# Two one-number tiles take 64-byte homes in a decoder block's SBUF

## The chip, the cores and the metric

The kernel runs on one core of a Trainium2 chip. The metric is the device time of one execution in microseconds (us), as the median of several runs. The kernel before takes 746.96 us (three runs, 746.91 to 747.18).

## What is computed

One decoder block for 512 tokens of width 1024, in float32, cut here to what matters:

```python
h = rms_norm(x, g_mix)
u, q, k, v, gate_logits = split(h @ w_in)              # 512, 512, 512, 512, 1024 columns
y_pool = causal_multiscale_pool(u, w_pool, pool_scale)
o = diff_attention(rope(q), rope(k), v, lam)           # 4 heads, two softmaxes each, subtracted
y_attn = rms_norm(o, g_subln) * (1.0 - lam_init)
x = x + (concat(y_pool, y_attn) * sigmoid(gate_logits)) @ w_out
x = x + memory_cross_attention(rms_norm(x, g_cross), rms_norm(mem, g_mem))   # 256 memory rows
x = x + square(relu(rms_norm(x, g_mlp) @ w_up)) @ w_down                     # 1024 -> 4096 -> 1024
return rms_norm(x, g_final)
```

## The kernel before, in words

Activations stand transposed, features on the 128 partitions and the 512 tokens along the free dimension. Every large product is made from a high and a low float32r part of each operand. `mm3(o, lh, ll, rh, rl)` issues three matmuls into one PSUM tile (L94, L95, L96): high times high, high times low, low times high. In `nc.tensor.matmul(o, a, b)`, `a` is the stationary block (128 x 128) that TensorE loads into its array, and `b` is the moving tile that streams through it (512 columns mostly, 256 in some stages). `tile_mm` makes one output tile of 128 features from eight blocks of the contraction, so with 24 matmuls. In the mixers' input projections, the output projections and the MLP, the stationary operands are weight blocks: loaded into `wraw` by DMA, split by ScalarE (L100) into `whi` and by VectorE (L101) into `wlo`, three buffers each, always ahead of use.

The moving operands have homes by stage:

- q, k, gates and pooling input (until 171 us): `xg`, the scaled input.
- output projection of the mixers (from 171 us): `mix`.
- keys from the memory, `mem_k`: the normed memory in tiles of the tag `s`, 256 columns wide. Values from the memory, `mem_v`, turn it round: `s` is stationary and the weight block `whi` or `wlo` moves.
- cross attention: the query projection moves `xg`; scores have `s` stationary and `mix` moving, 256 columns wide; the products with the values have `mix` stationary and `at` moving.
- its output projection: `xg`. The first half of each MLP group ("up", eight tiles, 192 matmuls): `mix`. The second half ("down", eight tiles, 192 matmuls): `xg`. There are four such groups, one after the other, to the end.

TensorE's instructions keep the order in which the code issues them. Tiles come from one pool. `sb(tag, shape, bufs)` gives a tag `bufs` homes in a row; the homes stand in order of first use, and each is rounded up to 32 bytes per partition. So a tile of one float takes 32 bytes, and moves all that stands behind it by 32. `eps` (one float, the bias of each norm's logarithm) stands behind `vx`, `cst` and `tmp`; `gsub` (one float per partition, a gain of the attention's norm) stands behind `vr` and `lam`. In the built program the first byte of each tag, within a partition, is:

```
tag           bytes of a home   before, mod 64   mod 128   after, mod 64   mod 128
cst, tmp      6912, 2048              0              64           0             64
eps           32 (after: 64)          0               0           0              0
one_f, ones   512                    32              96           0              0
ss, wraw      2048, 4096             32              96           0              0
xg            4096                   32              96           0              0
whi, wlo      4096                   32              96           0              0
rstd          2048                   32              96           0              0
vr            2048                   32              32           0             64
gsub          32 (after: 64)         32              32           0              0
s             4096                    0               0           0             64
at            8192                    0               0           0             64
mix           4096                    0               0           0             64
```

All homes of one of these tags share the remainder, and so do their halves and the 128-column blocks in them, since these are multiples of 512 bytes apart.

Of the kernel before, what the change touches and what calls it, by code (L numbers as in the profile page):

```python
# [17 lines left out]
P = 128  # L18
# [9 lines left out]
EPS = 1e-6  # L28
# [18 lines left out]
def block_kernel(ctx: ExitStack, tc: tile.TileContext, x0g, xT, memT, wv, wm, wckv, wpool, vecs, csts, outT):  # L47
# [14 lines left out]
    def nm(s):  # L62
        uid[0] += 1
        return f"{s}_{uid[0]}"

    def sb(tag, shape, bufs, dt=F32):
        return pool.tile(shape, dt, tag=tag, name=nm(tag), bufs=bufs)

    def tmp(dt=F32):
        return sb("tmp", [P, T], 10, dt)  # L70
# [7 lines left out]
    def ps(tag, bufs):  # L78
        return psum.tile([P, T], F32, tag=tag, name=nm(tag), bufs=bufs)
# [7 lines left out]
    V = nc.vector  # L87
# [25 lines left out]
    warm = ps("acc", 2)  # L113
    for j in range(WARM):
        nc.tensor.matmul(warm, idle[:, :P], idle, start=j == 0, stop=j == WARM - 1)
    eps = sb("eps", [P, 1], 1)
    V.memset(eps, EPS)
    one_f = sb("onef", [P, P], 1)
    V.memset(one_f, 1.0)
    ones = sb("ones", [P, P], 1, F32R)  # L120
    V.tensor_copy(ones, one_f)

# [1 line left out]
    blocks = []  # L124

    def add(src):
# [35 lines left out]
            prep(j)  # L162
        return ready.pop(i)

# [1 line left out]
    def rsqrt(dst, ssum, scale, v, l, by=None):  # L166
        """dst = (ssum * scale + EPS) ** -0.5, times by(y) for a first factor; v and l are scratch"""
        V.tensor_scalar(v, ssum, scale, EPS, op0=ALU.mult, op1=ALU.add)
        S.activation(l, ssum, AF.Ln, bias=eps, scale=scale)
        S.activation(dst, l, AF.Exp, scale=-0.5)  # L170
        S.activation(l, dst, AF.Square)
        V.scalar_tensor_tensor(l, l, -0.5, v, op0=ALU.mult, op1=ALU.mult)
        if by is not None:
            by(dst)
        V.scalar_tensor_tensor(dst, l, 1.5, dst, op0=ALU.add, op1=ALU.mult)
# [38 lines left out]
        S.activation(hi, src, AF.Copy, scale=g)  # L214
        V.scalar_tensor_tensor(lo, src, g, f(hi), op0=ALU.mult, op1=ALU.subtract)

# [1 line left out]
    clock = [0]  # L218
    due = []

# [24 lines left out]
                first and n == 0, last and n == len(ks) - 1)  # L245
            tick()

# [1 line left out]
    WU, WQ, WK, WGATE, WOUT, WCQ, WCO = 0, 4, 8, 12, 20, 28, 36  # L249
    WUP = 44  # L250
    WDN = WUP + 32
# [25 lines left out]
    def W(*key):  # L277
        return weights(where[key])

# [1 line left out]
    xr = {0: vx[:, NG_COL:]}  # L281
    xg = {}
    ss = sb("ss", [P, T], 1)
# [18 lines left out]
            load(k // 2)  # L302
    nc.sync.dma_start(cst, csts)

# [1 line left out]
    def lambdas():  # L306
        lvec = tmp()[:, :NVEC]
        nc.gpsimd.dma_start(lvec, vecs)
        lam = sb("lam", [P, 4], 1)
        lsum = sb("lsum", [P, 4], 1)  # L310
        for j in range(2):
            b = 128 * j
            V.tensor_tensor(lvec[:, b:b + 64], lvec[:, b:b + 64], lvec[:, b + 64:b + 128], op=ALU.mult)
            V.tensor_reduce(lsum[:, j:j + 1], lvec[:, b:b + 64], axis=AX.X, op=ALU.add)
            S.activation(lam[:, j:j + 1], lsum[:, j:j + 1], AF.Exp)
        V.tensor_tensor(lam[:, 2:3], lam[:, 0:1], lam[:, 1:2], op=ALU.subtract)
        V.tensor_scalar(lam[:, 3:4], lam[:, 2:3], LAM_INIT, None, op0=ALU.add)
        gsub = sb("gsub", [P, 1], 1)
        V.tensor_scalar(gsub, vec[:, GSUB:GSUB + 1], 1.0 - LAM_INIT, None, op0=ALU.mult)
        st["lam"], st["gsub"] = lam[:, 3:4], gsub  # L320

# [1 line left out]
    def v_proj():  # L323
        o = [ps("sc", 3), ps("sc", 3), ps("sc", 3), ps("av", 1)]
        tbs = [slice(i * P, (i + 1) * P) for i in range(NT)]
        for b in range(4):
            wh, wl = W("v", b)
            for kk in range(2):
                k = 2 * b + kk
                if k not in xg:  # L330
                    x_in(k)
                c = slice(kk * T, (kk + 1) * T)
                for i, tb in enumerate(tbs):
                    nc.tensor.matmul(o[i], xg[k][0][:, tb], wh[:, c], start=k == 0, stop=False)  # L334
                for i, tb in enumerate(tbs):
                    nc.tensor.matmul(o[i], xg[k][1][:, tb], wh[:, c], start=False, stop=False)  # L336
                for i, tb in enumerate(tbs):
                    nc.tensor.matmul(o[i], xg[k][0][:, tb], wl[:, c], start=False, stop=k == KC - 1)  # L338
                accumulate(ss, k, xr[k])
        sp = split_sq(ss, T)  # L340

        def stats():
            r = rstd_full(sp, ss)
            st["rstd"] = r
            rr = rstd_rows(sp, NT)
            V.tensor_tensor(cos_r, cos_r, r, op=ALU.mult)
            V.tensor_tensor(sin_r, sin_r, r, op=ALU.mult)
            vs = []
            for i in range(NT):
                vh = sb("vr", [P, T], 8, F32R)  # L350
                vl = sb("vr", [P, T], 8, F32R)
                scaled(vh, vl, o[i], rr[:, 2 * i:2 * i + 1])
                vs.append((vh, vl))
            st["v"] = vs
            lambdas()

        after(3, stats)

# [1 line left out]
    def qk_proj(which, h):  # L360
        o = acc()
        tile_mm(o, W(which, h), xg)
        a, b = tmp(), tmp()
        for j in range(4):
            S.copy(b[32 * (j ^ 1):32 * (j ^ 1) + 32, :], o[32 * j:32 * j + 32, :])  # L365
        V.tensor_tensor(a, o, cos_r, op=ALU.mult)
        ROPE_E.tensor_tensor(b, b, sin_r, op=ALU.mult)
        nc.gpsimd.tensor_tensor(a, a, b, op=ALU.add)
        s = pair("s", 6)
        top, bot = slice(0, 64), slice(64, 128)  # L370
        S.copy(s[top, 0, :], a[top, :])
        V.tensor_tensor(s[bot, 0, :], a[top, :], f(s[top, 0, :]), op=ALU.subtract)
        S.copy(s[bot, 1, :], a[bot, :])
        V.tensor_tensor(s[top, 1, :], a[bot, :], f(s[bot, 1, :]), op=ALU.subtract)
        st[which, h] = s
        if which == "k":
            z = pair("s", 6)
            nc.sync.dma_start(f(z[top, :, :]), f(s[bot, :, :]))
            nc.sync.dma_start(f(z[bot, :, :]), f(s[top, :, :]))
            st["z", h] = z  # L380

# [1 line left out]
    def scores(h, i):  # L383
        q, k, z = st["q", h], st["k", h], st["z", h]
        n = P * (i + 1)
# [50 lines left out]

        after(FINISH, finish)

# [1 line left out]
    gate, mixed, pooled = {}, {}, {}  # L440

    def gate_proj(m):
# [18 lines left out]
        split(pr[:, 0, :], pr[:, 1, :], y, MLO_E if m < 4 else V)  # L461
        mixed[m] = (pr[:, 0, :], pr[:, 1, :])

# [1 line left out]
    def pool_weights():  # L465
        r = sb("wraw", [P, D], 3)[:, :T]
        nc.sync.dma_start(r, wpool)
# [44 lines left out]
                after(START + SPACE * j, scores, j // NT, j % NT)  # L512
        tiles[kind](m)

# [1 line left out]
    res = {}  # L516

    def residual(m, o, g=None, ss=None, nxt=None, tag=None):
# [23 lines left out]
            tile_mm(o, W(key, m), rhs, early + late)  # L542
            done(m, o)

# [1 line left out]
    def mem_in():  # L546
        mg = {}
        sm = sb("ssm", [P, M], 1)
# [44 lines left out]
            scaled(p[:, 0, :], p[:, 1, :], o[i], st["mrow"][:, 2 * i:2 * i + 1])  # L593
            st["mv", half, i] = (p[:, 0, :], p[:, 1, :])

# [1 line left out]
    ss1 = sb("ss", [P, T], 1)  # L597
    x1g = {}

# [15 lines left out]

    after(STAT1, stats1)

# [1 line left out]
    cross_o = {}  # L619

    def cross_scores(h):
# [81 lines left out]

    after(STAT2, stats2)

# [1 line left out]
    ss3 = sb("ss", [P, T], 1)  # L707
    y3 = {}

    def last_rows(m, o, c):  # L710
        """Columns c of the last residual tile, then the final norm of those tokens."""
        w = c.stop - c.start
        V.tensor_tensor(res[m][:, c], o[:, c], res[m][:, c], op=ALU.add)
        sq = tmp()[:, :w]
        S.activation(sq, res[m][:, c], AF.Square)
        S.activation(y3[m // 2][:, 1, c], res[m][:, c], AF.Copy, scale=vec[:, G_FINAL + m:G_FINAL + m + 1])  # L716

        def norm():
            s = ps("tr", 2)[:, :w]
            nc.tensor.matmul(s, ones, st["sp3"][0][:, c], start=True, stop=False)  # L720
            nc.tensor.matmul(s, ones, st["sp3"][1][:, c], start=False, stop=False)
            nc.tensor.matmul(s, one_f, sq, start=False, stop=True)
            r, v, l = tmp()[:, :w], tmp()[:, :w], tmp()[:, :w]
            with tc.high_priority():
                S.activation(l, s, AF.Ln, bias=eps, scale=1.0 / D)
                S.activation(r, l, AF.Exp, scale=-0.5)
                V.tensor_scalar(v, s, 1.0 / D, EPS, op0=ALU.mult, op1=ALU.add)
                V.tensor_tensor(l, r, r, op=ALU.mult)
                V.scalar_tensor_tensor(l, l, -0.5, v, op0=ALU.mult, op1=ALU.mult)
                V.scalar_tensor_tensor(r, l, 1.5, r, op0=ALU.add, op1=ALU.mult)  # L730
            for j in range(KC // 2):
                for i in range(2):
                    eng = G if 2 * j + i in ON_POOL[c.start > 0] else V
                    eng.tensor_tensor(y3[j][:, i, c], y3[j][:, i, c], r, op=ALU.mult)  # L734
                nc.sync.dma_start(outT[:, 2 * j:2 * j + 2, c], y3[j][:, :, c])

        after(4, norm)

    for g in range(NG):
# [10 lines left out]
        for m in range(KC):  # L750
            last = g == NG - 1
# [3 lines left out]
            if last and m == KC - 1:  # L755
                st["sp3"] = split_sq(ss3, T)
                for hf, o in enumerate((ps("sc", 3), ps("sc", 3))):
                    c = slice(hf * M, (hf + 1) * M)
# [7 lines left out]
            if last:  # L766
                accumulate(ss3, m, res[m])
                S.activation(y3[m // 2][:, m % 2, :], res[m], AF.Copy,
                             scale=vec[:, G_FINAL + m:G_FINAL + m + 1])
# [70 lines left out]
```

## Time and profile before

| | |
|---|---|
| median of 3 runs | 746.96 us (746.91 to 747.18) |
| profiled execution, first to last instruction (span) | 744.6 us |
| what lies around the span, median less span | 2.4 us |
| TensorE (PE) busy | 726.1 us, 98% |
| VectorE (DVE), ScalarE (ACT), GpSimd (POOL) busy | 430.2, 354.9, 58.7 us |
| granted TensorE clock | 0.99 of full speed |

The profiled execution has no separate total beside its span; the runs' times are those of the first row. A matmul's busy time is longer than its share of the work, since matmuls overlap in the array: what counts is the distance from one matmul's start to the next one's start, which the timeline shows.

### The profile page before, as it was taken

To read this page: it belongs to the slowest core of one execution; us is meant where nothing else is said; L and a number is where in the kernel's file an instruction comes from. 1 tells how busy PE (TensorE), PEld (TensorE's weight loads), DVE (VectorE), ACT (ScalarE), POOL (GpSimd) and SP (SyncE) were. 2 spreads that over 40 slices of the span, in tenths; PEclk is the share of its full clock that TensorE was granted. 3 is DMA by queue.
4 is the path that set the end of the run, shared out by engine and by line. 5 is a ranking of instruction groups with operands and counts; after the bars stand their busy time and mean duration, and the time that the engine had idled before them with its cause. 6 is when DMAs were issued, how large, how long until landed. Compare 5 with 4: busy or idle time off the path is not lost.

```text
span 744.6 us, 8888 instructions
## 1 busy us (share of the span) xinstructions
PE 726.1 (98%) x3384; PEld 598.4 (80%) x3384; DVE 430.2 (58%) x677; ACT 354.9 (48%) x589; POOL 58.7 (8%) x50
## 2 busy tenths in 40 slices
PE   8999999999999999999999999999999999999993
PEld 6878888788889888888888888888888888888882
DVE  7587899875978556564664433443334533345436
ACT  7498997776765435344453411333214422234332
POOL 0053113533000000000000000000000000000003
PEclk9999999999999999999999999999999999999997
DMA  8343223241535531201323223233232232222203
GB/s 320 132 124 103 85 72 113 86 165 62 189 99 188 181 136 58 85 29 42 129 85 111 87 89 110 85 92 106 85 112 86 85 112 86 97 101 86 85 0 113
DMA packets 24650, 78.41 MB, mean 105 GB/s; under 512 B 2688, under 2 KB 4736, under 8 KB 24608
## 3 DMA queue, kind: packets, MB, share of 16 engines
q1 hardware_dynamic: 24560, 77.73, 32.0%
q8 instruction: 26, 0.43, 0.3%
q14 instruction: 16, 0.13, 0.1%
q0 software_dynamic: 48, 0.13, 0.0%
HBM read 73.65 MB, written 2.10 MB: 102 GB/s over the span
## 4 chain that ended last, share of the span: by engine, by line
PE 88%; ACT 5%; DVE 4%; DMA 1%; issue 1%; POOL 0%; SPq 0%; DVEq 0%; ACTq 0%
PE acc L94 25%; PE acc L96 24%; PE acc L95 24%; PE sc L96 3%; PE sc L94 3%; PE sc L95 3%; ACT tmp L395 1%; DVE mix L734 1%; DMA tmp<-xT 1%; ACT whi L100 1%; PE sc L334 1%; PE sc L336 1%; PE sc L338 1%; ACT tmp L365 1%; DVE tmp L393 1%
## 5 line engine op out<-in xcount | busy, mean ns | idle before, releaser
L100 ACT CAST whi<-wraw 128x1024 fp32r<-128x1024 f32 (+1 forms) x128 | 133.9, 1047 | 301.6 <-PE acc L95 233.2
L94 PE MATMUL acc<-xg,whi 128*128 128x512 f32 x504 | 198.6, 394 | 0.0
L96 PE MATMUL acc<-xg,wlo 128*128 128x512 f32 x504 | 196.7, 390 | 0.0
L95 PE MATMUL acc<-xg,whi 128*128 128x512 f32 x504 | 196.2, 389 | 0.0
L101 DVE TENSOR_TENSOR wlo<-wraw,whi 128x1024 fp32r<-128x1024 f32 (+1 forms) x128 | 158.2, 1236 | 32.3 <-ACT whi L100 31.2
L94 PE MATMUL acc<-mix,whi 128*128 128x512 f32 x296 | 117.0, 395 | 0.0
L96 PE MATMUL acc<-mix,wlo 128*128 128x512 f32 x296 | 116.9, 395 | 0.0
L95 PE MATMUL acc<-mix,whi 128*128 128x512 f32 x296 | 116.9, 395 | 0.0
L96 PEld LDWEIGHTS acc<-xg,wlo 128*128 128x128 f32 x504 | 94.6, 188 | 20.2
L94 PEld LDWEIGHTS acc<-xg,whi 128*128 128x128 f32 x504 | 94.7, 188 | 19.0
L95 PEld LDWEIGHTS acc<-xg,whi 128*128 128x128 f32 x504 | 94.7, 188 | 18.7
L520 DVE TENSOR_TENSOR vr<-acc,vr 128x512 f32<-128x512 f32 x41 | 28.3, 691 | 109.6 <-PE acc L96 109.6
L745 DVE SCALAR_TENSOR_TENSOR tmp<-acc,rstd 128x512 f32<-128x512 f32 x32 | 22.2, 693 | 87.6 <-PE acc L96 87.5
L96 PEld LDWEIGHTS acc<-mix,wlo 128*128 128x128 f32 x296 | 55.5, 187 | 13.6
L94 PEld LDWEIGHTS acc<-mix,whi 128*128 128x128 f32 x296 | 55.5, 187 | 13.5
L95 PEld LDWEIGHTS acc<-mix,whi 128*128 128x128 f32 x296 | 55.5, 187 | 13.5
L734 POOL TENSOR_TENSOR mix<-mix,tmp 128x256 f32<-128x256 f32 x7 | 6.1, 903 | 552.1 <-ACT mix L716 550.9
L101 DVE TENSOR_TENSOR xg<-tmp,xg 128x512 fp32r<-128x512 f32 x32 | 22.1, 692 | 0.3 <-ACT xg L100 0.3
L395 ACT ACTIVATE tmp<-tmp,small 128x128 f32<-128x128 f32 (+3 forms) x32 | 17.9, 560 | 5.8 <-DVE small L393 5.6
L100 ACT CAST xg<-tmp 128x512 fp32r<-128x512 f32 x32 | 19.8, 621 | 0.9
L746 ACT ACTIVATE tmp<-tmp 128x512 f32<-128x512 f32 x32 | 20.2, 633 | 0.0
L211 DVE TENSOR_TENSOR ss<-ss,tmp 128x512 f32<-128x512 f32 x27 | 18.5, 686 | 1.6 <-ACT tmp L210 1.4
(229 smaller groups left out, 945.1 us busy)
## 6 DMA issues: line engine op xcount, KB each, us to landing
wraw<-wm SPq DMA_DIRECT2D x108, 512.0 KB, 3.3
wraw<-wckv SPq DMA_DIRECT2D x16, 512.0 KB, 3.9
s<-s SPq DMA_DIRECT2D x8, 256.0 KB, 3.6
vr<-xT SPq DMA_DIRECT2D x8, 256.0 KB, 4.8
outT<-mix SPq DMA_DIRECT2D x8, 256.0 KB, 2.2
tmp<-xT SPq DMA_DIRECT2D x7, 256.0 KB, 6.7
wraw<-wv SPq DMA_DIRECT2D x3, 512.0 KB, 7.0
tmp<-memT SPq DMA_DIRECT2D x4, 256.0 KB, 4.7
```

The source lines that it names most:

```text
L94: nc.tensor.matmul(o, lh, rh, start=start, stop=False)
L95: nc.tensor.matmul(o, lh, rl, start=False, stop=False)
L96: nc.tensor.matmul(o, ll, rh, start=False, stop=stop)
L100: S.copy(hi, src)
L101: eng.tensor_tensor(lo, src, f(hi), op=ALU.subtract)
L211: V.tensor_tensor(ss, ss, sq, op=ALU.add)
L334: nc.tensor.matmul(o[i], xg[k][0][:, tb], wh[:, c], start=k == 0, stop=False)
L395: S.activation(e[:, :n], e[:, :n], AF.Exp, bias=mn, scale=-1.0, accum_out=sm[:, c:c + 1])
L520: V.tensor_tensor(t, o, t, op=ALU.add)
L734: eng.tensor_tensor(y3[j][:, i, c], y3[j][:, i, c], r, op=ALU.mult)
L745: V.scalar_tensor_tensor(t, o, 0.0, st["r2"], op0=ALU.max, op1=ALU.mult)
L746: S.activation(t, t, AF.Square)
```

## The change

Two tiles are allocated with sixteen floats per partition and used by their first one. Their values and all instructions stay as they are: on every engine, the program's instructions stand in the same order. The tiles behind `eps` move up by 32 bytes, and those behind `gsub` by 64. The other lines of the diff take out comments and docstrings.

```diff
-    eps = sb("eps", [P, 1], 1)
+    eps = sb("eps", [P, 16], 1)[:, :1]
     V.memset(eps, EPS)
...
-        gsub = sb("gsub", [P, 1], 1)
+        gsub = sb("gsub", [P, 16], 1)[:, :1]
         V.tensor_scalar(gsub, vec[:, GSUB:GSUB + 1], 1.0 - LAM_INIT, None, op0=ALU.mult)
```

## Rows read from the trace of the kernel before

**Rows 1.** The page: span, busy time by engine, shares of the last-ending chain.
```profile
span 744.6 us, 8888 instructions
PE 726.1 (98%) x3384; PEld 598.4 (80%) x3384; DVE 430.2 (58%) x677; ACT 354.9 (48%) x589; POOL 58.7 (8%) x50
PE 88%; ACT 5%; DVE 4%; DMA 1%; issue 1%; POOL 0%; SPq 0%; DVEq 0%; ACTq 0%
```
**Rows 2.** Windows (length, busy by engine, PEclk, DMA share, GB/s): attention, then MLP halves.
```profile
55.00:110.00 55.00, 53.60 (x258) 43.98 (x258) 46.65 (x110) 50.79 (x109) 12.45 (x10) 1.00 0.30 92
110.00:165.00 55.00, 53.93 (x258) 44.55 (x259) 47.93 (x112) 40.73 (x83) 21.57 (x16) 1.00 0.34 107
...
421.50:465.10 43.60, 43.60 (x194) 36.06 (x193) 16.00 (x17) 9.64 (x11) 0.00 (x0) 1.00 0.30 97
465.10:509.90 44.80, 44.80 (x194) 35.99 (x193) 20.02 (x23) 16.58 (x23) 0.00 (x0) 1.00 0.30 94
```
**Rows 3.** Timeline (start, length, engine, line): first matmuls of MLP halves, and one later.
```profile
421.51 0.40 PE L94 MATMUL acc<-xg,whi 128*128 128x512 f32 x1
...
423.14 0.39 PE L95 MATMUL acc<-xg,whi 128*128 128x512 f32 x1
...
465.07 0.40 PE L94 MATMUL acc<-mix,whi 128*128 128x512 f32 x1
...
509.87 0.40 PE L94 MATMUL acc<-xg,whi 128*128 128x512 f32 x1
```
**Rows 4.** Timeline: one matmul, and the weight load that starts with it.
```profile
499.84 0.40 PE L96 MATMUL acc<-mix,wlo 128*128 128x512 f32 x1
499.84 0.19 PEld L94 LDWEIGHTS acc<-mix,whi 128*128 128x128 f32 x1
```
**Rows 5.** Timeline: the output projection's first three tiles; `mem_v`, first row and next stage's first.
```profile
171.24 0.40 PE L94 MATMUL sc<-mix,whi 128*128 128x512 f32 x1
...
188.05 0.39 PE L94 MATMUL acc<-mix,whi 128*128 128x512 f32 x1
...
239.81 0.39 PE L94 MATMUL sc<-whi,s 128*128 128x512 f32 x1
...
262.21 0.39 PE L94 MATMUL sc<-xg,whi 128*128 128x512 f32 x1
```
**Rows 6.** Timeline: cross attention, products with the values.
```profile
323.66 0.39 PE L95 MATMUL acc<-at,mix 128*128 128x512 f32 x1
...
325.25 0.39 PE L96 MATMUL acc<-at,mix 128*128 128x512 f32 x1
```
**Rows 7.** Timeline: `mem_k`, one of its rows; cross scores, two rows, seven matmuls apart.
```profile
223.13 0.28 PE L95 MATMUL acc<-s,whi 128*128 128x256 f32 x1
...
319.34 0.28 PE L94 MATMUL sc<-mix,s 128*128 128x256 f32 x1
...
320.18 0.28 PE L95 MATMUL sc<-mix,s 128*128 128x256 f32 x1
```
**Rows 8.** Timeline: places where one operand gives way to another.
```profile
155.79 0.40 PE L94 MATMUL tr<-tmp,s 128*128 128x512 f32 x1
156.03 0.39 PE L95 MATMUL tr<-tmp,s 128*128 128x512 f32 x1
...
156.26 0.40 PE L96 MATMUL tr<-tmp,s 128*128 128x512 f32 x1
...
156.95 0.39 PE L96 MATMUL acc<-xg,wlo 128*128 128x512 f32 x1
157.18 0.39 PE L94 MATMUL av<-at,vr 128*128 128x512 f32 x1
...
316.00 0.40 PE L96 MATMUL acc<-xg,wlo 128*128 128x512 f32 x1
316.24 0.39 PE L94 MATMUL acc<-at,mix 128*128 128x512 f32 x1
```
**Rows 9.** Waits from 335 to 724 us: who waited for whom, total, times, longest.
```profile
ACT whi L100 <- PE acc L95: 218.7, 59, 4.5
DVE vr L520 <- PE acc L96: 103.7, 34, 3.4
DVE tmp L745 <- PE acc L96: 87.5, 31, 3.5
```

## The prediction, made before the changed kernel ran

> **What bounds the kernel now.** I read the page first. TensorE is busy 726.1 of 744.6 us and holds 88% of the chain that ended last; no other engine is busy for more than 58% [rows 1]. [...] The table of waits agrees: from 335 us on the long waits are those of ScalarE and VectorE for TensorE [rows 9]. [...]
>
> The change touches no instruction, only addresses, so the question is whether TensorE's pace depends on addresses. The timeline answers it, read from start to start. An MLP group has two halves with equal counts: 192 matmuls of 512 columns with the same weight homes `whi` and `wlo`. The "down" half, which moves `xg`, lasts from 421.51 to 465.07: 43.56 us, **226.9 ns** a matmul. The "up" half, which moves `mix`, lasts from 465.07 to 509.87: 44.80 us, **233.3 ns** [rows 3]. TensorE is without a gap in both [rows 2]. What differs is the moving tile's home. While a matmul streams its moving tile, the stationary block of the next one is loaded: a load starts at 499.84 together with a matmul [rows 4]. So two tiles are read at a time, and I sort all pairs (moving tile; stationary block of the next matmul) by the remainders in the table of homes:
>
> - `xg` with `whi`, both 32 past a multiple of 64: 226.9.
> - `at` with `mix`, both at a multiple of 64: seven matmuls from 323.66 to 325.25, 1.59 us, 227 [rows 6].
> - `mix` (0) with `whi` (32): 233.3 in the MLP; 72 matmuls in 16.81 us in the output projection, 233.5 [rows 3, 5].
> - `whi` (32) moving with `s` (0) stationary, in `mem_v`: 96 matmuls in 22.40 us, 233.3 [rows 5].
>
> Like remainders give 227, unlike ones 233, whichever side is at 32 and whatever the stage's other work is. I take this as the mechanism: a pair of unlike remainder costs about 6.4 ns per 512-column matmul. It is not the 32 itself that costs, since `xg` with `whi` has it on both sides.
>
> **The change part by part.** After it, every tag in the table is at 0 modulo 64, so all these pairs are alike. I price each stage by the pace of the like pair.
>
> 1. MLP up halves: four, each from 44.80 to the down half's 43.56: 4 x 1.24 = **-4.96 us**.
> 2. Output projection of the mixers: 192 matmuls, 233.5 to 226.9: **-1.27**.
> 3. `mem_v`: 96 matmuls, 233.3 to 226.9: **-0.61**.
> 4. `mem_k` goes the other way. Its 256-column matmuls, now an unlike pair (`s` with `whi`), run at 116.7 ns: 143 of them from 223.13 to 239.81, in 16.68 us [rows 5, 7]. The cross scores, a like pair (`mix` with `s`) of the same width, run at 120.0: seven from 319.34 to 320.18 [rows 7]. So 192 matmuls should lose 3.3 ns each: **+0.63**.
> 5. Changes of pair. After an unlike pair the pace needs some matmuls to settle: the first seven of a down half, 421.51 to 423.14, take 1.63 us, against 7 x 0.227 = 1.59 [rows 3]. Some ten such places lie behind 165 us, at 0.02 to 0.04 us: **-0.3**. What follows transposes and other short matmuls stays.
> 6. Attention, 53 to 165 us: about 28 places (16 scores, 4 products with the values, 4 norms, 4 pooling products) change the pair at 0.02 to 0.05 us each, so up to 1.0 us. But the chain there also runs through ScalarE, which is nearly full [rows 2], so some of that only becomes waiting. Bounds 0 and 1.0; I take **-0.4**, a little under the middle.
>
> The sum is -4.96 - 1.27 - 0.61 + 0.63 - 0.3 - 0.4 = **-6.9 us**. Nothing in it waits for others: the down halves already run at the faster pace with the same weight traffic (97 GB/s, DMA share 0.30), and in the up halves VectorE and ScalarE are busy 20.02 and 16.58 of 44.80 us [rows 2], so weight splits stay ahead. The sixteen-float tiles cost no instruction, and the order on each engine is unchanged. Against the span of 744.6 that gives 737.7; the runs' median stands 2.4 above the span, so **740.1 us**, 0.9% faster. With term 6 at its ends and the paces read a tenth of a us per stage off, the likeliest case itself spans 739.0 to 741.0.
>
> The weak point is the step from "64" to "alike". Behind the change `mix`, `s` and `at` are at 64 modulo 128, and `xg`, `whi`, `wlo` and `ones` at 0: the pairs that were 32 apart become 64 apart modulo 128, not equal. All of the long stretches above with a pace of 227 have pairs equal modulo 128 too, so they can't tell a period of 64 from one of 128. Pairs that are 64 apart already stand at two kinds of place. At 156.95 `xg` (96) moves while `vr` (32) is loaded, and the matmul takes 0.23, as a like pair does; where `xg` moves while `mix` (0) is loaded, 316.00 to 316.24, it takes 0.24 [rows 8]. That speaks for a period of 64. The four pooling products move `tmp` (64) while `s` (0) is loaded: of one, two steps take 0.24 and 0.23 [rows 8]; but they follow directly on an unlike pair, where a like pair hasn't settled either. So the long-run pace at 64 apart is unmeasured. Its bounds from the nearest rows are 227 (like) and 240 (the slowest step seen, 155.79 to 156.03); I take 227, by the one place that is not disturbed from before.
>
> [...] The rows show that TensorE's pace with weight loads behind it takes two values by the homes of the two tiles [rows 3, 5, 6]. [...]
>
> **Rivals.**
>
> - *Homes don't matter, something else about the stage does* (the squares and splits that run beside the up half, say: VectorE 20.02 us there against 16.00). Then the change does nothing: 747.0, with `mem_k` not slower either. For it: the up half does have more work beside it [rows 2]. Against it: `mem_v` has the slow pace with quite other work, and `at` with `mix` the fast one [rows 5, 6]. Chance 0.04.
> - *The period is 128 or more*, and 64 apart is about as bad as 32 apart: 746 to 747.5. For it: the pooling steps at 0.24 and 0.23. Against it: the 0.23 at 156.95 [rows 8]. Chance 0.06.
> - *64 apart is worse than 32 apart*, the slower side. The price is decided by one number, the long-run pace of such a pair, and from 233.5 on the kernel gets slower. At the 240 that one step shows, 1056 matmuls (768 + 192 + 96) lose about 6.5 ns each, 6.9 us: 754. Chance 0.05.
> - *Partly alike*: the pairs settle between, at about 230, and half of the sum is left: 743.5. Chance 0.03.
>
> **How the numbers follow.** My forecast holds with a chance of 0.82: 740.1. The range 738.8 to 741.8 is its own with the bounds of term 6, of the settling and of `mem_k`'s price; what it leaves out is the rivals, just under 2 in 10. A measurement of this kernel can tell about 0.2%, 1.5 us, from no change. Faster takes the forecast and the partial case, 0.85; the same takes the first two rivals less what would fall just outside, 0.10; slower is 0.05.
>
> **What would show it.** In the changed kernel's timeline an up half should last 43.5 us, like a down half, which should stay at 43.5; `mem_v` 21.8 instead of 22.4; `mem_k` should run at 120 ns instead of 117; the weight loads, the other engines' instruction lengths and the DMA's should be as before. The forecast is wrong if the up halves stay at 44.8 (no effect, or a period over 64) or grow to 46 (64 apart is worse), or if the down halves slow down, which would say that 32 on both sides is better than 0 on both.

## The result

The changed kernel takes **742.16 us** (median of five runs, 742.07 to 742.97) against 747.10 (746.91 to 747.37) for the kernel before: a ratio of 0.9938, 95% interval 0.9925 to 0.9950. It is faster by 4.9 us, where 6.9 were forecast, and the time lies 0.4 us above the forecast range.

The page of the changed kernel, its span and busy times (before: [rows 1]):

```profile
span 741.0 us, 8888 instructions
PE 722.2 (97%) x3384; PEld 598.8 (81%) x3384; DVE 429.4 (58%) x677; ACT 354.6 (48%) x589; POOL 58.7 (8%) x50
```

TensorE lost 3.9 us of busy time and the span 3.6; the other engines kept their busy time to within 1 us. The windows of the same stretches as in [rows 2], attention, then a down and an up half:

```profile
55.70:110.70 55.00, 53.60 (x258) 44.02 (x258) 46.51 (x110) 50.74 (x109) 12.38 (x10) 1.00 0.30 92
...
420.40:463.90 43.50, 43.50 (x193) 36.04 (x192) 15.99 (x17) 9.56 (x10) 0.00 (x0) 1.00 0.30 97
463.90:507.90 44.00, 44.00 (x193) 36.06 (x193) 19.93 (x23) 16.54 (x23) 0.00 (x0) 1.00 0.30 96
```

The timeline, at the places of [rows 3, 5, 7]:

```profile
171.76 0.40 PE L94 MATMUL sc<-mix,whi 128*128 128x512 f32 x1
...
188.26 0.39 PE L94 MATMUL acc<-mix,whi 128*128 128x512 f32 x1
...
222.76 0.28 PE L95 MATMUL acc<-s,whi 128*128 128x256 f32 x1
...
239.60 0.40 PE L94 MATMUL sc<-whi,s 128*128 128x512 f32 x1
...
262.00 0.39 PE L94 MATMUL sc<-xg,whi 128*128 128x512 f32 x1
...
420.39 0.39 PE L94 MATMUL acc<-xg,whi 128*128 128x512 f32 x1
...
463.94 0.40 PE L94 MATMUL acc<-mix,whi 128*128 128x512 f32 x1
...
507.90 0.40 PE L94 MATMUL acc<-xg,whi 128*128 128x512 f32 x1
```

Each length is the difference of two starts. The up half is now 507.90 - 463.94 = 43.96 us, 229.0 ns a matmul: neither the 233.3 of before nor the 226.9 of the down half (43.55, as before). The output projection's 72 matmuls take 16.50 us, 229.2 ns. `mem_v` still takes 22.40 us, 233.3 ns. `mem_k`'s 143 matmuls take 16.84 us, 117.8 ns, one more than before; the stage's first 48, ahead of these, run at 113.3 ns instead of 116.7, so that the whole stage loses only 0.08 us. The time came from the pairs of `mix` with `whi`, and only two thirds of what was expected of them.

### The profile page after: what moved, and what is told of

Read it like the earlier page. It is cut to its first block, busy times and chain, and to the rows that moved or that the text cites. A ratio compares the mean times of both kernels' runs of the same rounds, so it can differ in the third digit from the quotient of the medians.

```text
span 741.0 us, 8888 instructions
## 1 busy us (share of the span) xinstructions
PE 722.2 (97%) x3384; PEld 598.8 (81%) x3384; DVE 429.4 (58%) x677; ACT 354.6 (48%) x589; POOL 58.7 (8%) x50
## 4 chain that ended last, share of the span: by engine, by line
PE 87%; DVE 5%; ACT 4%; DMA 1%; issue 1%; POOL 0%; SPq 0%; DVEq 0%; ACTq 0%
PE acc L94 25%; PE acc L96 24%; PE acc L95 24%; PE sc L94 3%; PE sc L96 3%; PE sc L95 3%; ACT tmp L395 1%; DMA tmp<-xT 1%; DVE mix L734 1%; DVE tmp L393 1%; PE sc L334 1%; ACT tmp L365 1%; PE sc L336 1%; PE sc L338 1%; ACT whi L100 1%
## 5 line engine op out<-in xcount | busy, mean ns | idle before, releaser
L94 PE MATMUL acc<-mix,whi 128*128 128x512 f32 x296 | 116.3, 393 | 0.0
L95 PE MATMUL acc<-mix,whi 128*128 128x512 f32 x296 | 115.2, 389 | 0.0
```

The lines of the kernel that those rows point to most:

```text
L94: nc.tensor.matmul(o, lh, rh, start=start, stop=False)
L95: nc.tensor.matmul(o, lh, rl, start=False, stop=False)
```

## The experiments

Theory A, formed on this: what sets the pace is the *distance* between the first byte of the moving tile and that of the next stationary block, with a period longer than 64 bytes. ("Next" is argued from [rows 4]; in all these runs a matmul's own stationary block has the same remainder as the next one, so they can't tell the two apart.) Before, `mix` stood 32 past `whi`; now it stands 64 past it. The rivals: B, each tile gains by standing at a multiple of 64 itself; C, the period is 64 after all, and the 229 ns come from the work beside the up half.

Each ratio below is to the kernel before, run beside it (medians 746.88 to 747.03).

**Each tile alone.** First without the change to `gsub`:

```diff
-        gsub = sb("gsub", [P, 16], 1)[:, :1]
+        gsub = sb("gsub", [P, 1], 1)[:, :1]
```

> Only the first of the two tiles is widened: weights and xg come to multiples of 64, while s, at and mix come to 32 past one. The pair of mix with whi is again 32 apart, as before the change. Theory A (a pair's pace depends on the distance between the two homes, with a period of more than 64 bytes; equal homes are best, 64 apart is between): the up halves of the MLP last 44.8 us again and the time is that of before, 746.5 to 747.5. Theory B (each tile that stands at a multiple of 64 gains by itself): the weights' part of the gain stays, 743 to 745.

Measured: 746.82 us, ratio to before 0.9997 (0.9989 to 1.0006). An up half, first matmul and first one after it, lasts 44.81 us, as before:

```profile
465.00 0.40 PE L94 MATMUL acc<-mix,whi 128*128 128x512 f32 x1
...
509.81 0.40 PE L94 MATMUL acc<-xg,whi 128*128 128x512 f32 x1
```

Then without the change to `eps`:

```diff
-    eps = sb("eps", [P, 16], 1)[:, :1]
+    eps = sb("eps", [P, 1], 1)[:, :1]
```

> Only the second tile is widened: all tiles that TensorE reads in the long stages stand 32 past a multiple of 64, none at one, and mix with whi are 64 apart as after the change. Theory A: the distances are those of the changed kernel, so the up halves last 44.0 us and the time is 741.7 to 742.7. Theory B: no tile stands at a multiple of 64, so 746.5 to 747.5 or slower.

Measured: 742.39 us, ratio 0.9935 (0.9923 to 0.9947). An up half of this kernel in the timeline, first matmul and first one after it:

```profile
463.20 0.40 PE L94 MATMUL acc<-mix,whi 128*128 128x512 f32 x1
...
507.16 0.40 PE L94 MATMUL acc<-xg,whi 128*128 128x512 f32 x1
```

That is 43.96 us, to the last digit the changed kernel's, though here every tile of the long stages stands 32 past a multiple of 64. So the gain is the second tile's, B falls, and multiples of 64 have nothing to do with it.

**The disputed pace by itself.** A kernel of nothing but matmuls, in segments, moves one tile against a fixed one:

```python
for n, (w, o) in enumerate(segments):        # columns, shift in floats
    for j in range(48):
        c = slice((j % 8) * P, (j % 8) * P + P)
        nc.tensor.matmul(acc[:, :w], stat[:, c], move[:, o:o + w], start=j == 0, stop=j == 47)
```

> No decoder block is computed, only a sweep: segments of 48 matmuls with the same eight stationary blocks, the moving tile's start shifted by a number of bytes against them, 512 columns (0 to 496 in steps of 16, and 4, 8, 512, 576, 768, 1024), then 256 columns (0 to 480 in steps of 32). Theory A: with nothing beside TensorE, 226.7 ns at distance 0, 229 at 64, 233.4 at 32, 192 and 224 (the distances of the long stages), and the same again a period further on; the period shows in the table, at most 512. With 256 columns 120 at 0 and about 117 at 32 and 320. Theory C: 226.7 at every multiple of 64.

Beside TensorE there is only VectorE's copy of each finished tile, and TensorE is busy from its first matmul on without a gap, 527.0 us. Two windows (columns as in [rows 2], without ScalarE), each from one start to the 24th start after it, at distance 32 and at 64; the counts include matmuls that are still ending:

```profile
50.51:56.11 5.60, 5.60 (x26) 4.50 (x25) 0.00 (x0) 0.00 (x0) 1.00 0.00 0
72.81:78.30 5.49, 5.49 (x25) 4.51 (x24) 0.00 (x0) 0.00 (x0) 1.00 0.00 0
```

The table is worked out from the starts in its trace, the mean of the last 24 steps of each segment (to the next segment's first start), in ns, by distance in bytes:

```
512 columns   0      16     32     48     64     80     96     112
              226.7  231.7  233.3  233.3  228.9  231.1  233.3  231.1
              128    144    160    176    192    208    224    240
              232.1  233.3  234.5  233.3  233.3  234.5  233.3  226.7
              256 to 496: each as the one 256 bytes before, within 0.1; 512, 768, 1024: 226.7; 576: 228.9
256 columns   0      32     64     96     128    160    192    224
              120.0  117.8  117.8  120.0  118.6  118.7  117.8  118.3
```

For homes at multiples of 32, theory A stands, with a period of 256 bytes: 226.7 at 0, 228.9 at 64 (the changed kernel's `mix` with `whi`), 233.3 at 32 and at 224 (the pairs of before), and 233.3 at 192, which is where the change put `mem_v`: there the weight block moves and `s` is stationary, so the distance is -64, which is 192 modulo 256. C falls: at multiples of 64 the pace is 226.7, 228.9, 232.1 and 233.3, with next to nothing beside TensorE.

**Equal homes in the kernel.** If only the distance counts, the kernel gets the rest by equal remainders modulo 256:

```diff
-        return sb("small", [P, 4], 24)[:, :n]
+        return sb("small", [P, 4], 32)[:, :n]
...
-        gsub = sb("gsub", [P, 16], 1)[:, :1]
+        gsub = sb("gsub", [P, 64], 1)[:, :1]
```

> The second tile takes 256 bytes and the tag small has 32 homes instead of 24, so that s, at and mix have the same remainder modulo 512 as xg, whi and wlo. Theory A: all long pairs are equal and run at 226.7 ns, mem_v too; up halves 43.5 us (4 x 0.45 less than after the change), output projection 0.45 and mem_v 0.65 less, mem_k 0.6 more: about 2.3 us less than the changed kernel, 739.5 to 740.5. Theory C (a period of 64, and the 229 ns of the pair of mix with whi after the change comes from something else in the up half, such as the work beside it): as the changed kernel, 742.2.

Measured: 740.53 us, ratio 0.9910 (0.9896 to 0.9924). Timeline of the end of `mem_k`, of `mem_v`, and an up half:

```profile
239.45 0.40 PE L94 MATMUL sc<-whi,s 128*128 128x512 f32 x1
...
261.24 0.39 PE L94 MATMUL sc<-xg,whi 128*128 128x512 f32 x1
...
462.65 0.39 PE L94 MATMUL acc<-mix,whi 128*128 128x512 f32 x1
...
506.17 0.39 PE L94 MATMUL acc<-xg,whi 128*128 128x512 f32 x1
```

The up half is 43.52 us, 226.7 ns, and `mem_v` 21.79, 227.0; `mem_k` runs at 120.0 ns and loses 0.5 us, as the forecast had it for like pairs.

**A control and a loss on demand.** The first takes the changed kernel and only the 32 homes of `small`, which moves `mix` and `at` by 256; the second puts `mix` at one of the slow distances:

```diff
-        gsub = sb("gsub", [P, 16], 1)[:, :1]
+        gsub = sb("gsub", [P, 40], 1)[:, :1]
```

> The changed kernel with 32 homes instead of 24 for the tag small, which alone moves at, gate and mix by 256 bytes. Theory A with a period of 256: every distance keeps its remainder (mix stands 320 past whi, which is 64), so up halves of 44.0 us and the time of the changed kernel, 741.7 to 742.7; the eight more homes cost or give nothing. With a period of 512, or if the homes of small were what made the kernel with equal homes faster: 740.5 or another value off 742.2.

> The second tile takes 160 bytes, so mix stands 160 past whi modulo 256, the distance with one of the slowest paces of the sweep (234.46 ns). The whole kernel's tiles stand at multiples of 32 only. Theory A, with the sweep's table: an up half 192 x 0.2345 = 45.0 us (before: 44.8), the output projection 0.2 more than before, mem_k at 118.7 ns 0.4 more, mem_v (distance 96) as before at 233.3: about 1.4 us slower than before, 748.0 to 748.8. Theory C (only the remainder modulo 64 counts, and 32 is as bad as it gets): as before, 747.0.

Measured: 742.75 us (0.9940, 0.9927 to 0.9954) with up halves of 43.96, so the period of 256 holds in the kernel too and the homes of `small` give nothing by themselves. And 748.92 us (1.0022, 1.0014 to 1.0031) for the distance of 160, slower than before. Its up half:

```profile
466.04 0.40 PE L94 MATMUL acc<-mix,whi 128*128 128x512 f32 x1
...
511.02 0.40 PE L94 MATMUL acc<-xg,whi 128*128 128x512 f32 x1
```

44.98 us, 234.3 ns, where the sweep's table said 234.5. Three of these times miss their forecast ranges, by 0.03 us (740.53), 0.05 (742.75) and 0.12 (748.92); the up halves came as forecast. The change could as well have made the kernel slower; nothing in "a multiple of 32" or "of 64" tells.

**A finer sweep.**

> No decoder block is computed, only a sweep in segments of 40 matmuls: distance 0 to 252 bytes in steps of 4 with 512 columns; 0 to 240 in steps of 16 with 256 columns; both tiles shifted by the same 16, 32, 64 and 128 bytes, at distance 0 and at 32; stationary blocks of 96, 64 and 32 columns at distance 0 and 32; 384 and 128 moving columns at distance 0, 32 and 64. Theory A: shifting both changes nothing (226.7 and 233.3). [...]

In steps of 4 bytes the pace goes from 226.7 to 240.0 (at 132, 196 and 244) and never under 226.7, which comes at 0, 28, 60, 108, 156 and 252; 240, which gave 226.7 in the first sweep, gave 236.7 here, so the distance doesn't fix the pace everywhere. At multiples of 32, the only homes that the kernel's tiles can have, the two sweeps agree to 1.2 ns with 512 columns. Both tiles shifted by 32, 64 or 128 keep their pace at distance 0 (227.0, 226.6, 226.7); shifted by 16 they do not (233.2), so below 32 bytes the distance alone isn't enough. With 384 columns the pace is 173.3 at 0, 32 and 64, with 128 columns 111.7 at all three: no difference shows among these three. With 96, 64 and 32 stationary columns the pace is 230.0, 230.0 and 231.7 ns at distance 0, and 227.0, 231.0 and 233.4 at distance 32; with 96 columns 32 is the faster distance. So the pace neither falls in step with what the weight load reads nor stays the same: at distance 0 it goes from 226.7 ns with 128 stationary columns to 230.0 with 96 and 231.7 with 32.

**Homes chosen by the table.** Last, `mix` and `at` equal to `whi` modulo 256, and `s` 192 past it, where the first sweep's 256 columns go faster (117.8 ns, against 120.0 at 0):

```diff
-        return sb("small", [P, 4], 24)[:, :n]
+        return sb("small", [P, 4], 26)[:, :n]
...
-        gsub = sb("gsub", [P, 16], 1)[:, :1]
+        gsub = sb("gsub", [P, 48], 1)[:, :1]
```

> Homes chosen by the sweeps' tables: mix and at equal to whi modulo 256, s at 192 past whi, by padding the second tile to 192 bytes and giving small 26 homes. Theory A: the up halves and the output projection run at 226.7 ns as with equal homes; mem_k (distance 192, 256 columns) at 117.8 or, if it locks as in the fine sweep, at 113.3 instead of 120.0, 0.4 to 1.3 us less; mem_v (distance 64) at 228.9 instead of 226.7, 0.2 more; cross scores at 117.8 instead of 120.0, 0.2 less: 0.4 to 1.3 us less than the kernel with equal homes, 739.2 to 740.2. If only the tables of 512 columns carry over to the kernel, 740.7.

> The kernel with equal homes modulo 512 again, beside the kernel with homes chosen by the table on the same chip. Theory A: 740.1 to 741.0, with mem_k at 120.0 ns and mem_v at 226.9.

Measured: 739.69 us (0.9901, 0.9888 to 0.9914), and 740.21 (0.9917, 0.9903 to 0.9931) for equal homes beside it. The intervals overlap, so the times don't settle the half microsecond between them; the stages do. In this kernel's timeline `mem_k`'s second row of the place in [rows 7], the ends of `mem_k` and `mem_v`:

```profile
222.65 0.28 PE L95 MATMUL acc<-s,whi 128*128 128x256 f32 x1
...
238.90 0.39 PE L94 MATMUL sc<-whi,s 128*128 128x512 f32 x1
...
260.87 0.40 PE L94 MATMUL sc<-xg,whi 128*128 128x512 f32 x1
```

143 matmuls in 16.25 us, 113.6 ns (with equal homes 120.0); `mem_v` 21.97 us, 228.9. Both versions stand below the changed kernel's 742.16, and the interval of the one chosen by the table lies wholly below that of the changed kernel.

## Why the prediction was wrong

What bounds the kernel, and that the homes of the two tiles read together set TensorE's pace, was right: the rival in which homes don't matter fell with the first two experiments (up halves of 44.81 and 43.96 us). A weight load and a matmul start together at 499.84 [rows 4], and in the sweeps the pace with 512 columns goes from 226.7 to 240.0 ns with nothing changed but a home. Whether it is the load that costs the time, and why, stayed open.

The step that failed is the one named as the weak point, from "64" to "alike": every tag comes to 0 modulo 64, "so all these pairs are alike", and are priced at the pace of equal homes, "I take 227, by the one place that is not disturbed from before." In its place the runs showed a period of 256: 64 apart, `mix` with `whi` ran at 229.0 ns, and `mem_v`, at 192, at 233.3 as before. The choice rested on a single matmul at 156.95 (0.23 in [rows 8], 226 ns in the trace). The sweep shows why one matmul can't carry it: at a distance of 64 the steps run 230, 226, 230, 232, 225, 230, 232, so a step of 226 is among the slow pair's own. The pooling product's steps of 0.24 and 0.23, just as short a sequence, could not have decided it either, and they stand at another distance: adding up the homes in the code gives, before, modulo 256, `xg` at 224 and `vr` at 160, which is 64 apart, but `tmp` at 192 and `s` at 0. (By the same count `eps` stands at 64 modulo 128, and `gsub` at 96 before, not at 0 and 32 as the table of homes has it; TensorE reads neither.) The case that came closest was "partly alike", with a chance of 0.03.

That the kernel got two thirds of the gain was luck: by the reasoning put on record, `mix` 128 or 192 past `whi` would have been as good, and the sweep has 232.1 and 233.3 there, against 233.3 before the change.

The terms, from the starts of the stages in both profiles and in the kernel with equal homes, the last row ending at the first scores (us, against before):

```
                              forecast   changed kernel   equal homes
1 MLP up halves                 -4.96       -3.37            -5.11
2 output projection             -1.27       -0.81            -1.22
3 mem_v                         -0.61        0.00            -0.61
4 mem_k                         +0.63       +0.08            +0.53
5 settling, cross and down      -0.3        -0.01            -0.28
6 attention, 54 to 171 us       -0.4        -0.10            -0.12
  up to 54 us                    0          +0.62            +0.45
```

Terms 1 to 5 are right for equal homes, to 0.15 us each, and were applied to homes that are not equal. Term 6 was too large, even there. Part of it may be that its pairs weren't made equal: with equal homes `tmp` still stands 192 past `s`, as before, and `at` 64 past `vr`. Whether that is why, or attention's chain through ScalarE (busy 50.74 of 55 us in its first half) kept what TensorE gave, no run separates. The last row isn't shown to be the change's. The V projection's first stretch waits for loads (ScalarE for `tmp<-xT` 1.30 us in the kernel before, 2.10 in the changed one), and its length differs by 0.9 us among nine profiles; the kernel with `gsub` alone, which has the changed kernel's long pairs, reaches the scores 0.27 us earlier than the kernel before. But two profiles of the kernel with equal homes reach them within 0.01 us of each other, so what sets this row stays open. The five runs of the changed kernel have spans of 740.1 to 741.0 us; the profiled one, of 742.82, has the longest, and the median run's is 740.2, which is part of why the profiled spans differ by only 3.6 us.

## What to carry to other kernels

Where TensorE's busy share is near 1 (98% here), compare the step from start to start between stages of equal shape; two values for the same shape, here 226.9 and 233.3 ns, say that something other than work sets the pace, and the homes of the tiles are one thing to look at. Sweep the quantity before trusting a round number: "multiples of 64" was true of the changed kernel and had no part in its gain, and a rule that held here for 512 columns, equal remainders modulo 256 for the moving tile and the stationary blocks, gave 0.2% to 0.3% more for the same kind of edit. One row at 226 in a sequence that wanders between 225 and 232 is not a price.

## What the hardware showed that I hadn't expected

The pace of matmuls of 512 float32r columns depends on the distance of two homes, from 226.7 ns to 240.0; at distances in steps of 16 bytes it repeated after 256 bytes in the first sweep, within 0.1 ns. With 256 columns the same distances order otherwise: 0, one of the best with 512 columns (226.7), is among the slowest (120.0), and a segment can keep one of two paces at the same distance (117.8 in one sweep and 113.3 in the other at 192; 116.7 in the kernel before and 117.8 in the one with `eps` alone, both at 32). Inside one kernel, the one with homes by the table, `mem_k`'s first 48 matmuls ran at 117.8 and its last 72 at 113.3, all at 192. With 384 and with 128 columns no difference showed among the three distances tried (173.3 and 111.7 ns). What in the chip makes the period, and what picks one of two paces, stays open.
